# Sliding-window attention in steps of two query blocks, with the low key parts in the two row halves of TensorE

## The chip, the cores and the metric

The kernel runs on one core of one Trainium2 chip. The metric is the device time of one execution in microseconds (us), from its start to its end. The engines are named as in the profile: PE is TensorE (matrix products), PEld its loading of stationary operands ("weights"), DVE is VectorE, ACT is ScalarE, POOL is GpSimd, SP issues DMA transfers. PSUM is the memory that TensorE writes; it has eight banks of 512 float32 columns on 128 partitions. SBUF is the working memory that feeds the engines.

## The reference, cut to what matters

One transformer layer (D = 2048, 512 tokens): a root-mean-square norm, sliding-window attention with a gate, an output projection, then a second gated projection and a last norm. The change is inside the attention, which the reference computes per block of 128 queries against its own block of keys and the one before:

```python
q, k, v, gate = split(rmsnorm(x) @ w_in)     # 32 heads of q, 4 heads of k and v, 64 wide
scores = einsum('bnqhgd,bnjhd->bnhgqj', q, kb) * 64 ** -0.5 + bias
scores = where(mask, scores, min)            # 0 <= distance < 128
m = max(scores.max(-1), sink)
e = exp(scores - m)
probs = e / (e.sum(-1) + exp(sink - m))
out = einsum('bnhgqj,bnjhd->bnqhgd', probs, vb)
y = (out * silu(gate)) @ w_out
```

All of it is float32. The kernel gets close to that precision from products at the faster float32r rate by splitting each operand in a high part (rounded) and a low part (the rest), and adding the products high x high, low x high and high x low.

## The kernel before, in words

**Projections.** For each tile of 128 output columns, `mm3` (L113 to L115) runs three matmuls of 512 columns on each of 16 slices of D; three matmuls are one *projection slot*. `projections` (L592) is a generator that hands out one slot at a time: 30 tiles of q and of the gate, written to PSUM tag `p` (tiles qps and gps). The weights arrive by DMA in pieces of eight slices (wraw), ScalarE makes the high part whi (L99), VectorE the low part wlo (L100). When a tile of the gate is done, VectorE writes it to `gate` (L609); after four of them ScalarE applies silu (L404), which reloads its function table before and after.

**Attention in between.** Heads go in pairs (16 pairs c, of which four share a kv head), tokens in four blocks n. One step `i` is one pair and one block: 64 steps. The main loop (L631) runs `scores(i)`, then about seven projection slots, and `steps` (L621) puts `turn(i-1)` ahead of slot 4 and `weigh(i-2)` ahead of slot 6. The order on TensorE and of SP's transfers is the program's order; on the other engines a scheduler orders instructions by priority and data when the program is built, and each engine then runs its list in that order.

- `scores` (L304): for each head e of the pair, Q[c][e] holds that head's high part in one half of the 128 rows and its low part in the other half (even head: high in rows 0-63, odd head: high in rows 64-127). K holds the keys' high part in both halves, and the low part likewise. So one matmul of 128 rows against the high keys gives (high + low) q times high k. A second one against the low keys gives (high + low) q times low k. For block 0 there is one matmul of 256 columns per head (high and low side by side, L319), for blocks 1 to 3 two matmuls per head (L317). VectorE adds the bias (L326, sc), folds the two key blocks by a maximum (L332, t; exactly one of the two is unmasked at each position), takes the maximum over the row with the sink beside it (L337, sm); ScalarE takes the exponential with its sum (L340), VectorE divides (L341, L342). POOL writes the sink's column (L321).
- `turn` (L345): TensorE transposes t (L352, pt); ScalarE and VectorE split it in high and low (L354, L355: r); POOL cuts out the part that belongs to the query's own block (L360: own).
- `weigh` (L366): products with the values (L379); every second block ScalarE and VectorE combine the result to U (L385 to L388). POOL multiplies U into the gate later (L401, `gate_value`).

**Buffers.** PSUM has four tags p, s, t, o of two banks each. The scores use s, two buffers of one bank. In SBUF, t and sm have four buffers, r and own two.

**Weight sums.** `sum_weights` issues, a few in each step, copies (SP, L448) and adding copies (POOL queue, L450) that prepare sums of the later weights in DRAM.

**After the attention** the output projection begins (tiles o, banks s and p for the first product). Its weight pieces are split by ScalarE (L490, bhi) and VectorE (L491, blo), and VectorE combines quarters of `gate` (L572) for its operands.

Of the kernel before, what the change touches and what calls it, by code (L numbers as in the profile page):

```python
# [11 lines left out]
F32 = mybir.dt.float32  # L12
F32R = mybir.dt.float32r
# [36 lines left out]
def trunk_kernel(ctx: ExitStack, tc: tile.TileContext, a: dict):  # L50
    nc = tc.nc

    def pool(name, bufs=1, **kw):
        return ctx.enter_context(tc.tile_pool(name=name, bufs=bufs, **kw))
# [12 lines left out]
    acts = pool("acts", bufs=KC // 2)  # L67
    mid = ExitStack()
    more = mid.enter_context(tc.tile_pool(name="more", bufs=KC // 2))

    def quarter(name):
        return whole.tile([P, 4, S], F32, tag="quarter", name=name)

    def bank(name, tag):
        return psum.tile([P, 512], F32, tag=tag, name=name)


    WE = 1024
# [1 line left out]
    class Weights:  # L80
# [5 lines left out]
        def add(self, src):  # L86
            self.srcs.append(src)
# [204 lines left out]

    U, T, PT, O, gates, biases = {}, {}, {}, {}, {}, {}

    def load_bias(c):
# [3 lines left out]
        )  # L301
        nc.sync.dma_start(biases[c], src)

    def scores(i):  # L304


        c, n = divmod(i, NB)
        kv, nk = c // 4, 2 if n else 1
        if n == 0 and c + 1 < PAIRS:
            load_bias(c + 1)  # L310
        s_ps = bank(f"s{i}", "s").rearrange("p (u j) -> p u j", u=2)
        keys = slice(n + 1 - nk, n + 1)
        for e in range(2):
            st = Q[c][e][:, n * P : (n + 1) * P]
            if n:
                for low in range(2):
                    nc.tensor.matmul(s_ps[:, e, :], st, K[kv][:, keys, low], start=low == 0, stop=low == 1)  # L317
# [3 lines left out]
        nc.gpsimd.tensor_copy(t[:, :, 0], sinkb[:, 2 * c : 2 * c + 2])  # L321
        pr = t[:, :, 1:]
        sc = pr if n == 0 else apool.tile([P, 2, 2 * P], F32, tag="sc", name=f"sc{i}", bufs=1)

        def add(in0, in1):
            nc.vector.scalar_tensor_tensor(  # L326
                out=sc, in0=in0, scalar=sclq[:, n : n + 1], in1=in1, op0=ALU.mult, op1=ALU.add
            )

        if n:  # L330
            add(s_ps, biases[c][:, :, ::-1])
            nc.vector.tensor_max(pr, sc[:, :, :P], sc[:, :, P:])  # L332
        else:
            add(s_ps[:, :, :P], biases[c][:, :, :P][:, :, ::-1])
            add(s_ps[:, :, P:], sc)
        sm = apool.tile([P, 6], F32, tag="sm", name=f"sm{i}", bufs=4)
        nc.vector.tensor_reduce(sm[:, 0:2], t, axis=AX.X, op=ALU.max, negate=True)  # L337
        for e in range(2):
            te = t[:, e, :]
            nc.scalar.activation(te, te, AF.Exp, bias=sm[:, e : e + 1], accum_out=sm[:, 2 + e : 3 + e])  # L340
        nc.vector.reciprocal(sm[:, 4:6], sm[:, 2:4])  # L341
        nc.vector.tensor_mul(pr, pr, sm[:, 4:6].unsqueeze(2).to_broadcast([P, 2, P]))  # L342
        T[i] = t

    def turn(i):  # L345


        c, n = divmod(i, NB)
        t = T.pop(i)
        pt = bank(f"pt{i}", "t").rearrange("p (b u q) -> p b u q", b=2, u=2)[:, 0]  # L350
        for e in range(2):
            nc.tensor.transpose(pt[:, e, :], t[:, e, 1:], ident)  # L352
        r = apool.tile([P, 2, 2, P], F32R, tag="r", name=f"r{i}", bufs=2)
        nc.scalar.copy(r[:, 0], pt)  # L354
        nc.vector.tensor_sub(r[:, 1], pt, r[:, 0].bitcast(F32))  # L355
        own = None
        if n:
            own = apool.tile([P, 2, 2, P], F32R, tag="own", name=f"own{i}", bufs=2)
            flat = lambda v: v.rearrange("p l u q -> p (l u) q")
            nc.gpsimd.affine_select(  # L360
                out=flat(own), in_=flat(r).bitcast(F32), pattern=[[0, 4], [1, P]], compare_op=ALU.is_ge, fill=0.0,
                base=0, channel_multiplier=-1,
            )
        PT[i] = (r, own)

    def weigh(i):  # L366

        c, n = divmod(i, NB)
        kv = c // 4
        r, own = PT.pop(i)  # L370
        if n == 0:
            U[c] = apool.tile([P, S], F32, tag="u", name=f"u{c}", bufs=5)
        if n % 2 == 0:
            O[c] = bank(f"o{i}", "o").rearrange("p (b u q) -> p b u q", b=2, u=2)
        ops = O[c]
        parts = [(V[max(n - 1, 0)][:, kv], r)] + ([(DV[n][:, kv], own)] if n else [])
        for b, (st, pr) in enumerate(parts):
            for low in range(2):
                nc.tensor.matmul(  # L379
                    ops[:, n % 2], st, pr[:, low], start=b == low == 0, stop=low == 1 and b == len(parts) - 1  # L380
                )
        if n % 2 == 1:
            tmp = apool.tile([P, 2, P], F32, tag="tmp", name=f"tmp{i}", bufs=2)
            dst = U[c][:, (n - 1) * P : (n + 1) * P].rearrange("p (b q) -> p b q", b=2)
            nc.scalar.copy(tmp[0:64], ops[64:128, :, 0, :])  # L385
            nc.vector.tensor_add(dst[0:64], ops[0:64, :, 0, :], tmp[0:64])
            nc.scalar.copy(tmp[64:128], ops[0:64, :, 1, :])
            nc.vector.tensor_add(dst[64:128], ops[64:128, :, 1, :], tmp[64:128])  # L388
        if n == 3:
            weighed.add(c)  # L390
            if c in open_gates:
                due.append(c)
# [155 lines left out]
    class Forms:  # L548
# [6 lines left out]
        def steps(self, p):  # L555

            self.made[p] = []
            for h in range(2):
                a11, a21 = self.q[h][:, :, :256], self.q[h][:, :, 256:]
                a12, a22 = self.q[2 + h][:, :, :256], self.q[2 + h][:, :, 256:]  # L560
                if self.nm == "o":
                    src, sub = {
                        1: (a11, None), 7: (a11, (a21, a11)), 2: (a12, None), 6: (a11, (a22, a11)),
                        5: (a21, (a21, a22)), 3: (a12, (a12, a11)), 4: (a22, None),
                    }[p]
                else:
                    src, sub = {
                        2: (a12, None), 7: (a21, (a21, a11)), 1: (a11, None), 6: (a21, (a22, a21)),
                        5: (a11, (a11, a21)), 3: (a12, (a12, a21)), 4: (a22, None),
                    }[p]  # L570
                if sub:
                    nc.vector.tensor_sub(src, *sub)  # L572
# [42 lines left out]
    load_bias(0)  # L615
    for _ in range(KC):
        next(proj)
    blocks = PAIRS * NB
# [12 lines left out]
    for i in range(blocks):  # L631
        todo = left // (blocks - i)
        left -= todo
        scores(i)
        steps(i, todo)
        for n in range(i * SUM_STEPS // blocks, (i + 1) * SUM_STEPS // blocks):
# [327 lines left out]
```

## Time and profile before

| | |
|---|---|
| median of 3 runs | 835.68 us (832.84 to 836.26) |
| the profiled execution's own time | 835.59 us |
| its span, first to last instruction | 833.9 us |
| granted TensorE clock over the span | 0.990 |
| share of the span that PE, DVE, ACT, POOL are busy | 97%, 72%, 54%, 17% |
| attention stage | about 85 to 480 us |

How to read the rows. A *group* row gives line, engine, operation, the tile written and the tiles read, the shape and the count; then the busy time in us, the mean duration of one in ns, and the idle time of the engine just ahead of them with what ended it. A *timeline* row gives start and duration in us; "x2" merges two instructions, and the brackets hold the idle time before. A *wait* row reads "who <- for whom: us in total, times, longest". A row by *windows* gives for a stretch its length, then the busy time of PE, PEld, DVE, ACT and POOL with their counts, the granted clock, the share of DMA and GB/s. Matmuls are pipelined: one begins before the one ahead has ended, so the distance between two starts is what a matmul costs a busy TensorE.

### The profile page before, as it was taken

To read this page: it belongs to the slowest core of one execution; us is meant where nothing else is said; L and a number is where in the kernel's file an instruction comes from. 1 tells how busy PE (TensorE), PEld (TensorE's weight loads), DVE (VectorE), ACT (ScalarE), POOL (GpSimd) and SP (SyncE) were. 2 spreads that over 40 slices of the span, in tenths; PEclk is the share of its full clock that TensorE was granted. 3 is DMA by queue.
4 is the path that set the end of the run, shared out by engine and by line. 5 is a ranking of instruction groups with operands and counts; after the bars stand their busy time and mean duration, and the time that the engine had idled before them with its cause. 6 is when DMAs were issued, how large, how long until landed. Compare 5 with 4: busy or idle time off the path is not lost.

```text
span 833.9 us, 11252 instructions
## 1 busy us (share of the span) xinstructions
PE 811.3 (97%) x3972; PEld 679.1 (81%) x3972; DVE 599.4 (72%) x950; ACT 448.2 (54%) x860; POOL 145.5 (17%) x233
## 2 busy tenths in 40 slices
PE   8999999999999899999999988999999999999985
PEld 7888788888888788888888877888888888888874
DVE  3547877668787577768777877766656877769794
ACT  5734444644454554435644544554668856557664
POOL 1100211322222331212511130020000020202002
PEclk9999999999999999999999999999999999999998
DMA  8853767848577766776795277798521996875423
GB/s 292 305 190 111 192 190 234 215 151 219 146 216 233 215 196 195 214 166 174 205 277 164 76 274 280 261 301 220 194 84 51 371 203 208 184 212 185 151 87 116
DMA packets 45993, 165.98 MB, mean 199 GB/s; under 512 B 5440, under 2 KB 9696, under 8 KB 42096
## 3 DMA queue, kind: packets, MB, share of 16 engines
q1 hardware_dynamic: 38432, 129.52, 44.2%
q0 software_dynamic: 6928, 34.69, 21.9%
q10 hardware_dynamic: 576, 1.05, 0.4%
q8 instruction: 31, 0.51, 0.2%
q14 instruction: 26, 0.21, 0.1%
HBM read 160.99 MB, written 46.19 MB: 248 GB/s over the span
## 4 chain that ended last, share of the span: by engine, by line
PE 87%; DVE 5%; ACT 3%; DMA 2%; issue 1%; POOL 1%; SPq 0%; ACTq 0%; DVEq 0%
PE qps L114 7%; PE qps L113 7%; PE qps L115 7%; PE gps L113 6%; PE gps L115 6%; PE gps L114 6%; PE o L114 6%; PE o L115 6%; PE g L113 5%; PE o L113 5%; PE g L114 5%; PE g L115 5%; PE o L379 3%; PE s L317 2%; PE pt L352 2%
## 5 line engine op out<-in xcount | busy, mean ns | idle before, releaser
L491 DVE TENSOR_TENSOR blo<-braw,bhi 128x1024 fp32r<-128x1024 f32 x80 | 99.2, 1241 | 40.6 <-ACT bhi L490 40.4
L490 ACT CAST bhi<-braw 128x1024 fp32r<-128x1024 f32 x80 | 84.0, 1050 | 57.7 <-PE o L115 27.0
L340 ACT ACTIVATE t<-t,sm 128x129 f32<-128x129 f32 x128 | 50.6, 397 | 105.5 <-DVE sm L337 105.3
L113 PE MATMUL gps<-xh,whi 128*128 128x512 f32 x256 | 103.1, 403 | 0.0
L115 PE MATMUL gps<-xh,wlo 128*128 128x512 f32 x256 | 100.4, 392 | 0.0
L114 PE MATMUL gps<-xl,whi 128*128 128x512 f32 x256 | 100.4, 392 | 0.0
L100 DVE TENSOR_TENSOR wlo<-wraw,whi 128x1024 fp32r<-128x1024 f32 x60 | 75.1, 1251 | 29.3 <-ACT whi L99 28.3
L113 PE MATMUL qps<-xh,whi 128*128 128x512 f32 x224 | 91.1, 407 | 0.0
L114 PE MATMUL o<-blo,fho 128*128 128x512 f32 x224 | 88.0, 393 | 2.8 <-DVE blo L491 2.8
L113 PE MATMUL o<-bhi,fho 128*128 128x512 f32 x224 | 88.4, 395 | 1.5 <-ACT bhi L490 1.5
L115 PE MATMUL qps<-xh,wlo 128*128 128x512 f32 x224 | 88.3, 394 | 0.0
L114 PE MATMUL qps<-xl,whi 128*128 128x512 f32 x224 | 88.3, 394 | 0.0
L115 PE MATMUL o<-bhi,flo 128*128 128x512 f32 x224 | 88.0, 393 | 0.0
L99 ACT CAST whi<-wraw 128x1024 fp32r<-128x1024 f32 x60 | 62.7, 1045 | 36.6 <-DMA wraw<-in_w_gate_in 17.2
L113 PE MATMUL g<-bhi,fhg 128*128 128x512 f32 x208 | 81.3, 391 | 0.0
L115 PE MATMUL g<-bhi,flg 128*128 128x512 f32 x208 | 81.0, 389 | 0.0
L114 PE MATMUL g<-blo,fhg 128*128 128x512 f32 x208 | 80.9, 389 | 0.0
L491 DVE TENSOR_TENSOR blo<-grown,bhi 128x1024 fp32r<-128x1024 f32 x38 | 46.5, 1223 | 21.7 <-ACT bhi L490 21.2
L115 PEld LDWEIGHTS gps<-xh,wlo 128*128 128x128 f32 x256 | 48.1, 188 | 10.7
L114 PEld LDWEIGHTS gps<-xl,whi 128*128 128x128 f32 x256 | 48.3, 189 | 7.0
L490 ACT CAST bhi<-grown 128x1024 fp32r<-128x1024 f32 x38 | 39.9, 1050 | 26.0 <-PE o L115 11.0
L113 PEld LDWEIGHTS gps<-xh,whi 128*128 128x128 f32 x256 | 48.2, 188 | 6.9
(189 smaller groups left out, 1722.6 us busy)
## 6 DMA issues: line engine op xcount, KB each, us to landing
wraw<-in_w_gate_in SPq DMA_DIRECT2D x32, 512.0 KB, 6.1
wraw<-in_w_q SPq DMA_DIRECT2D x28, 512.0 KB, 7.1
w_out<-in_w_out POOLq DMA_DIRECT2D x24, 512.0 KB, 6.8
braw<-in_w_out SPq DMA_DIRECT2D x24, 512.0 KB, 3.2
braw<-in_ple_gate SPq DMA_DIRECT2D x24, 512.0 KB, 4.3
w_out<-in_w_out SPq DMA_DIRECT2D x16, 512.0 KB, 7.3
ple_gate<-in_ple_gate SPq DMA_DIRECT2D x16, 512.0 KB, 7.7
ple_gate<-in_ple_gate POOLq DMA_DIRECT2D x16, 512.0 KB, 7.7
```

Of the source, the lines that this page charges most:

```text
L99: nc.scalar.copy(hi, raw)
L100: nc.vector.tensor_sub(lo, raw, hi.bitcast(F32))
L113: nc.tensor.matmul(ps, sh, mh, start=first, stop=False, skip_group_check=more)
L114: nc.tensor.matmul(ps, sh, ml, start=False, stop=False, skip_group_check=more)
L115: nc.tensor.matmul(ps, sl, mh, start=False, stop=last, skip_group_check=more)
L317: nc.tensor.matmul(s_ps[:, e, :], st, K[kv][:, keys, low], start=low == 0, stop=low == 1)
L340: nc.scalar.activation(te, te, AF.Exp, bias=sm[:, e : e + 1], accum_out=sm[:, 2 + e : 3 + e])
L352: nc.tensor.transpose(pt[:, e, :], t[:, e, 1:], ident)
L379: nc.tensor.matmul(ops[:, n % 2], st, pr[:, low], start=b == low == 0, stop=low == 1 and b == len(parts) - 1)
L490: nc.scalar.copy(hi, raw)
L491: nc.vector.tensor_sub(lo, raw, hi.bitcast(F32))
```

## The change

The attention goes in 32 steps ("windows" w) of one pair and two blocks of queries (h = 0: blocks 0 and 1, h = 1: blocks 2 and 3). About 14 projection slots lie between two calls of `scores`; `turn(w-1)` stays ahead of slot 4, `weigh(w-2)` moves to slot 1, and in the last step back to slot 6. The products with the low parts of the keys use only the high part of q: 64 of the 128 rows, the even head in rows 0-63 and the odd head in rows 64-127. The product low q times low k is thereby left out. The two heads of a pair write to two different banks, so a window's scores take two banks as one buffer (`two_banks`), half a bank for each head and block. The exponentials stay one for each head and block; the maximum, the reciprocal, the division, the transposes' reading and the cut for the own block are one instruction for two blocks. t and sm have two buffers of twice the size or more, r and own one of twice the size. PSUM's pool ends with the attention, and a second one (`psum_late`) serves what follows; in it banks go to tags in the order of first use, and a tile waits for the earlier users of its bank.

```diff
-    psum = pool("psum", bufs=2, space=PSUM)
+    psum = [mid.enter_context(tc.tile_pool(name="psum", bufs=2, space=PSUM))]
...
+    def two_banks(name):
+        return psum[-1].tile([P, 2, 512], F32, tag="s", name=name, bufs=1)
...
-    kt_ps = [bank(f"ktps{t}", "s") for t in range(2)]
+    kt_both = two_banks("ktps")
+    kt_ps = [kt_both[:, t] for t in range(2)]
...
-        s_ps = bank(f"s{i}", "s").rearrange("p (u j) -> p u j", u=2)
-        keys = slice(n + 1 - nk, n + 1)
-        for e in range(2):
-            st = Q[c][e][:, n * P : (n + 1) * P]
+        s_ps = two_banks(f"s{w}").rearrange("p u (b j) -> p u b j", b=2)
+        for b in range(2):
+            n = 2 * h + b
+            cols = slice(n * P, (n + 1) * P)
+            if n == 0:
+                for e in range(2):
+                    nc.tensor.matmul(s_ps[:, e, b, :], Q[c][e][:, cols], K[kv][:, 0], start=True, stop=True)
+                continue
+            keys = slice(n - 1, n + 1)
+            for e in range(2):
+                nc.tensor.matmul(s_ps[:, e, b, :], Q[c][e][:, cols], K[kv][:, keys, 0], start=True, stop=False)
+            for e in range(2):
+                half = slice(64 * e, 64 * e + 64)
+                nc.tensor.matmul(
+                    s_ps[:, e, b, :], Q[c][e][half, cols], K[kv][half, keys, 1], start=False, stop=True
+                )
...
-            if n:
-                for low in range(2):
-                    nc.tensor.matmul(s_ps[:, e, :], st, K[kv][:, keys, low], start=low == 0, stop=low == 1)
-            else:
-                nc.tensor.matmul(s_ps[:, e, :], st, K[kv][:, 0], start=True, stop=True)
-        t = apool.tile([P, 2, 1 + P], F32, tag="t", name=f"t{i}", bufs=4)
+        t = apool.tile([P, 2, 2, 1 + P], F32, tag="t", name=f"t{w}", bufs=2)
...
-        sm = apool.tile([P, 6], F32, tag="sm", name=f"sm{i}", bufs=4)
-        nc.vector.tensor_reduce(sm[:, 0:2], t, axis=AX.X, op=ALU.max, negate=True)
-        for e in range(2):
+        sm = apool.tile([P, 24], F32, tag="sm", name=f"sm{w}", bufs=2)
+        flat = t.rearrange("p b u j -> p (b u) j")
+        nc.vector.tensor_reduce(sm[:, 0:4], flat, axis=AX.X, op=ALU.max, negate=True)
+        for e in range(4):
...
-        r = apool.tile([P, 2, 2, P], F32R, tag="r", name=f"r{i}", bufs=2)
+        r = apool.tile([P, 2, 2, 2, P], F32R, tag="r", name=f"r{w}")
...
-            own = apool.tile([P, 2, 2, P], F32R, tag="own", name=f"own{i}", bufs=2)
+        own = apool.tile([P, 2, 2, 2, P], F32R, tag="own", name=f"own{w}")
...
-    def steps(i, todo):
+    def steps(w, todo, at):
         for n in range(todo):
-            if n == 6 and 2 <= i < blocks + 2:
-                weigh(i - 2)
-            if n == 4 and 1 <= i < blocks + 1:
-                turn(i - 1)
-            if n == 5 and due:
+            if n == at and 2 <= w < windows + 2:
+                weigh(w - 2)
+            if n == 4 and 1 <= w < windows + 1:
+                turn(w - 1)
+            if n in (6, 10) and due:
                 gate_value()
...
+        steps(w, todo, 1)
+        for n in range(w * SUM_STEPS // windows, (w + 1) * SUM_STEPS // windows):
             sum_weights(n)
-    steps(blocks, 7)
-    steps(blocks + 1, 7)
+    steps(windows, 7, 1)
+    steps(windows + 1, 7, 6)
...
     late = pool("late", reuse_waits="tile")
+    psum.append(pool("psum_late", bufs=2, space=PSUM, reuse_waits="tile"))
```

More of the change, by code (lines that the diff above doesn't have):

```diff
@@ L74, in bank @@
     def bank(name, tag):
-        return psum.tile([P, 512], F32, tag=tag, name=name)
+        return psum[-1].tile([P, 512], F32, tag=tag, name=name)
+    def two_banks(name):
+        return psum[-1].tile([P, 2, 512], F32, tag="s", name=name, bufs=1)
     WE = 1024
@@ L302, in load_bias, with scores, add @@
         nc.sync.dma_start(biases[c], src)
[L304 to L309, printed above, removed]
+    def scores(w):
+        c, h = divmod(w, 2)
+        kv = c // 4
+        if h == 0 and c + 1 < PAIRS:
             load_bias(c + 1)
-        s_ps = bank(f"s{i}", "s").rearrange("p (u j) -> p u j", u=2)
-        keys = slice(n + 1 - nk, n + 1)
-        for e in range(2):
-            st = Q[c][e][:, n * P : (n + 1) * P]
+        s_ps = two_banks(f"s{w}").rearrange("p u (b j) -> p u b j", b=2)
[15 more added lines that the diff above has]
+        t = apool.tile([P, 2, 2, 1 + P], F32, tag="t", name=f"t{w}", bufs=2)
+        nc.gpsimd.tensor_copy(t[:, :, :, 0], sinkb[:, 2 * c : 2 * c + 2].unsqueeze(1).to_broadcast([P, 2, 2]))
+        for b in range(2):
+            n = 2 * h + b
+            pr = t[:, b, :, 1:]
+            sc = pr if n == 0 else apool.tile([P, 2, 2 * P], F32, tag="sc", name=f"sc{w}_{b}", bufs=1)
+            def add(in0, in1):
+                nc.vector.scalar_tensor_tensor(
+                    out=sc, in0=in0, scalar=sclq[:, n : n + 1], in1=in1, op0=ALU.mult, op1=ALU.add
+                )
@@ L337, in scores @@
-        nc.vector.tensor_reduce(sm[:, 0:2], t, axis=AX.X, op=ALU.max, negate=True)
-        for e in range(2):
[L339 to L352, printed above, removed]
-        r = apool.tile([P, 2, 2, P], F32R, tag="r", name=f"r{i}", bufs=2)
+                add(s_ps[:, :, b, :], biases[c][:, :, ::-1])
@@ new lines, in scores @@
+                nc.vector.tensor_max(pr, sc[:, :, :P], sc[:, :, P:])
+            else:
+                add(s_ps[:, :, b, :P], biases[c][:, :, :P][:, :, ::-1])
+                add(s_ps[:, :, b, P:], sc)
+        sm = apool.tile([P, 24], F32, tag="sm", name=f"sm{w}", bufs=2)
+        flat = t.rearrange("p b u j -> p (b u) j")
+        nc.vector.tensor_reduce(sm[:, 0:4], flat, axis=AX.X, op=ALU.max, negate=True)
+        for e in range(4):
+            te = flat[:, e, :]
+            nc.scalar.activation(te, te, AF.Exp, bias=sm[:, e : e + 1], accum_out=sm[:, 4 + e : 5 + e])
@@ new lines, in scores, with turn @@
+        nc.vector.reciprocal(sm[:, 8:12], sm[:, 4:8])
+        nc.vector.tensor_mul(flat[:, :, 1:], flat[:, :, 1:], sm[:, 8:12].unsqueeze(2).to_broadcast([P, 4, P]))
+        T[w] = t
+    def turn(w):
+        t = T.pop(w)
+        pt = bank(f"pt{w}", "t").rearrange("p (b u q) -> p b u q", b=2, u=2)
+        for b in range(2):
+            for e in range(2):
+                nc.tensor.transpose(pt[:, b, e, :], t[:, b, e, 1:], ident)
+        r = apool.tile([P, 2, 2, 2, P], F32R, tag="r", name=f"r{w}")
@@ L364, in turn, with weigh @@
-        PT[i] = (r, own)
-    def weigh(i):
-        c, n = divmod(i, NB)
+        own = apool.tile([P, 2, 2, 2, P], F32R, tag="own", name=f"own{w}")
+        flat = lambda v: v.rearrange("p l b u q -> p (l b u) q")
+        nc.gpsimd.affine_select(
+            out=flat(own), in_=flat(r).bitcast(F32), pattern=[[0, 8], [1, P]], compare_op=ALU.is_ge, fill=0.0,
+            base=0, channel_multiplier=-1,
+        )
+        PT[w] = (r, own)
+    def weigh(w):
+        c, h = divmod(w, 2)
         kv = c // 4
-        r, own = PT.pop(i)
-        if n == 0:
+        r, own = PT.pop(w)
+        if h == 0:
@@ L372, in weigh @@
             U[c] = apool.tile([P, S], F32, tag="u", name=f"u{c}", bufs=5)
[L373 to L389, printed above, removed]
+        ops = bank(f"o{w}", "o").rearrange("p (b u q) -> p b u q", b=2, u=2)
@@ new lines, in weigh @@
+        for b in range(2):
+            n = 2 * h + b
+            parts = [(V[max(n - 1, 0)][:, kv], r)] + ([(DV[n][:, kv], own)] if n else [])
+            for i, (st, pr) in enumerate(parts):
+                for low in range(2):
+                    nc.tensor.matmul(
+                        ops[:, b], st, pr[:, low, b], start=i == low == 0, stop=low == 1 and i == len(parts) - 1
+                    )
+        tmp = apool.tile([P, 2, P], F32, tag="tmp", name=f"tmp{w}", bufs=2)
+        dst = U[c][:, 2 * h * P : (2 * h + 2) * P].rearrange("p (b q) -> p b q", b=2)
@@ L390, in weigh @@
+        nc.scalar.copy(tmp[0:64], ops[64:128, :, 0, :])
+        nc.vector.tensor_add(dst[0:64], ops[0:64, :, 0, :], tmp[0:64])
+        nc.scalar.copy(tmp[64:128], ops[0:64, :, 1, :])
+        nc.vector.tensor_add(dst[64:128], ops[64:128, :, 1, :], tmp[64:128])
+        if h == 1:
             weighed.add(c)
@@ L617, in trunk_kernel @@
         next(proj)
-    blocks = PAIRS * NB
+    windows = PAIRS * NB // 2
     left = KC * (len(kinds) - 1) - 14
-    def steps(i, todo):
+    def steps(w, todo, at):
         for n in range(todo):
-            if n == 6 and 2 <= i < blocks + 2:
-                weigh(i - 2)
-            if n == 4 and 1 <= i < blocks + 1:
-                turn(i - 1)
-            if n == 5 and due:
+            if n == at and 2 <= w < windows + 2:
[3 more added lines that the diff above has]
+            if n in (6, 10) and due:
                 gate_value()
             next(proj)
-    for i in range(blocks):
-        todo = left // (blocks - i)
+    for w in range(windows):
+        todo = left // (windows - w)
         left -= todo
-        scores(i)
-        steps(i, todo)
-        for n in range(i * SUM_STEPS // blocks, (i + 1) * SUM_STEPS // blocks):
+        scores(w)
+        steps(w, todo, 1)
+        for n in range(w * SUM_STEPS // windows, (w + 1) * SUM_STEPS // windows):
             sum_weights(n)
-    steps(blocks, 7)
-    steps(blocks + 1, 7)
+    steps(windows, 7, 1)
+    steps(windows + 1, 7, 6)
     for _ in proj:
```

18 lines of the change are left out of this document (removed).

## The prediction

> **What bounds the kernel now.** I read the page's busy times first, then TensorE's waits, then its timeline inside one step of the attention, then the timelines around the two places where it stops.
>
> ```profile
> PE 811.3 (97%) x3972; PEld 679.1 (81%) x3972; DVE 599.4 (72%) x950; ACT 448.2 (54%) x860; POOL 145.5 (17%) x233
> ...
> PEclk9999999999999999999999999999999999999998
> ...
> PE pt L352 <- DVE t L342: 3.9, 2, 2.9
> PE o L114 <- DVE blo L491: 2.8, 2, 2.1
> ...
> 90.00:281.00 191.00, 190.03 (x968) 159.46 (x967) 143.06 (x276) 90.88 (x236) 44.37 (x80) 1.00 0.73 205
> 281.00:290.00 9.00, 6.10 (x24) 4.80 (x23) 4.85 (x11) 5.09 (x14) 5.72 (x6) 0.81 0.79 186
> 290.00:478.00 188.00, 188.00 (x957) 158.02 (x956) 143.84 (x272) 91.76 (x235) 45.19 (x73) 1.00 0.66 185
> ```
>
> TensorE is busy 97% of the span at an almost full clock. In the attention stage (90 to 478 us) its row is filled (190.03 of 191.00, 188.00 of 188.00), while VectorE (143.06 of 191.00) and ScalarE have room. So in this stage a matmul slot removed is time saved, and work on the other engines costs nothing until TensorE waits for it. It stopped there only for the transposes (L352), twice.
>
> **The slots.** Busy times of matmuls overlap, so I price by distances between starts.
>
> ```profile
> 208.53 0.39 PE L115 MATMUL gps<-xh,wlo 128*128 128x512 f32 x1
> 208.75 0.40 PE L317 MATMUL s<-K,qe 128*128 128x256 f32 x2
> 208.99 0.40 PE L317 MATMUL s<-K,qo 128*128 128x256 f32 x2
> 209.23 0.39 PE L113 MATMUL gps<-xh,whi 128*128 128x512 f32 x1
> 209.46 0.39 PE L114 MATMUL gps<-xl,whi 128*128 128x512 f32 x1
> ...
> L317 PEld LDWEIGHTS s<-K,qe x96: 187/188/188, 90.2 to 461.3; 128*128 128x128 f32 x96
> L317 PE MATMUL s<-K,qe x96: 277/280/283, 90.4 to 461.4; 128*128 128x256 f32 x96
> ```
>
> Four score matmuls of one block take 209.23 - 208.75 = 0.48 us, that is 0.12 us each, and a 512-column matmul 0.23 us. The two qe matmuls (keys high, keys low) are the x2 in one row.
>
> **The change, part by part.**
>
> *Low parts in row halves.* Before, blocks 1 to 3 of each of the 16 pairs (48 blocks) run four full matmuls. After, two full ones and two that use 64 rows each, head 0 in rows 0-63 and head 1 in rows 64-127, into different banks. The instructions are as many; if the two halves run at the same time, one slot in four goes: 48 x 0.12 = 5.8 us less. Block 0 has no low matmul and stays. No row of the trace shows a matmul on half the rows. Its gain is bounded by 5.8 us (full overlap) and 0 (no overlap); I take full overlap, since the operands lie in disjoint rows and the outputs in different banks. The full-to-half change of the array, 48 times in and 48 times out, is not in the trace either. The nearest rows are the transposes, another mode of the array, between full matmuls:
>
> ```profile
> 200.01 0.39 PE L115 MATMUL qps<-xh,wlo 128*128 128x512 f32 x1
> 200.24 0.38 PE L352 MATMUL pt<-ident,t 128*128 128x128 f32 x2
> 200.38 0.48 PE L113 MATMUL qps<-xh,whi 128*128 128x512 f32 x1
> 200.69 0.39 PE L114 MATMUL qps<-xl,whi 128*128 128x512 f32 x1
> ```
>
> The first transpose starts 0.23 us after the matmul ahead of it, the usual slot, so going over costs nothing. From 200.24 to 200.69 pass 0.45 us, of which the L113 matmul has 0.23: two transposes cost 0.22 us, 0.11 each, and coming back shows no extra. I take 0 for a switch. The upper end comes from the rows of one matmul: it lasts 0.28 us but gives up its slot after 0.12, so a full emptying of the array costs 0.16 us; if the next weights can only load after that (load at 208.53, matmul at 208.75, less what its slot hides: 0.12), 0.28 us. Over 96 switches that is 15.4 to 26.9 us, kept for a rival.
>
> *Two blocks a step.* Four transposes stand together instead of two and two; at 0.11 each that is equal. Weighing (L379) keeps its matmuls. So TensorE has no other term but its stops.
>
> ```profile
> 282.37 0.39 PE L115 MATMUL qps<-xh,wlo 128*128 128x512 f32 x1
> 285.66 0.66 PE L352 MATMUL pt<-ident,t 128*128 128x128 f32 x2 [2.90 <-DVE t L342]
> 285.97 0.78 PE L113 MATMUL qps<-xh,whi 128*128 128x512 f32 x1
> ...
> 288.25 0.63 PE L115 MATMUL qps<-xh,wlo 128*128 128x512 f32 x1
> 288.68 0.50 PE L379 MATMUL o<-r,V 128*128 128x256 f32 x2
> ...
> 93.41 0.39 PE L115 MATMUL gps<-xh,wlo 128*128 128x512 f32 x1
> 94.77 0.41 PE L352 MATMUL pt<-ident,t 128*128 128x128 f32 x2 [0.97 <-DVE t L342]
> ```
>
> At 282 us the transposes wait 3.29 - 0.23 = 3.1 us for t, and the next six matmuls run at the slow clock (granted 0.81 in that stretch): 285.97 to 288.68 is 2.71 us against 6 x 0.23, 1.3 us more. At 93 us 1.1 us goes. Together 5.5 us. Before, t has 7 + 4 = 11 projection slots (three matmuls, 0.69 us each) from its scores to its transposes, 7.6 us; after, 14 + 4 = 18, 12.4 us, plus the matmuls between. The work is this:
>
> ```profile
> L326 DVE SCALAR_TENSOR_TENSOR sc<-s,sclq,bias 128x512 f32<-128x512 f32 x48 | 35.8, 746 | 11.7 <-PE s L317 11.2
> L332 DVE TENSOR_TENSOR t<-sc 128x256 f32<-128x256 f32 x48 | 24.5, 510 | 1.6
> L337 DVE TENSOR_REDUCE sm<-t 128x2 f32<-128x258 f32 x64 | 27.0, 422 | 3.3 <-DVE t L326 0.5
> L342 DVE TENSOR_TENSOR t<-t,sm 128x256 f32<-128x256 f32 x64 | 28.7, 449 | 1.7
> L340 ACT ACTIVATE t<-t,sm 128x129 f32<-128x129 f32 x128 | 50.6, 397 | 105.5 <-DVE sm L337 105.3
> L340 ACT ACTIVATION_READ_ACCUMULATOR t<-t,sm 128x1 f32 x128 | 23.9, 187 | 0.0
> L360 POOL TENSOR_SCALAR_AFFINE_SELECT own<-r 128x512 fp32r<-128x512 f32 x48 | 33.6, 699 | 70.8 <-DVE r L355 70.8
> ...
> 278.00 1.28 ACT L404 ACT_TABLE_LOAD   x1
> 279.30 1.92 ACT L404 ACTIVATE gate<-gate 128x2048 f32<-128x2048 f32 x1
> 281.24 1.28 ACT L340 ACT_TABLE_LOAD   x1
> ```
>
> For two blocks at most 2 x (0.75 + 0.51 + 0.42 + 0.45) = 4.3 us of VectorE and four exponentials of 0.4 us (with their accumulator reads some 2.3 us), 6.6 us in line; the silu that held ScalarE for 4.5 us at 278 makes it 11.1, still under 12.4. I count both stops as gone: -5.5 us, with 0 as the other end, since weights that land late could hold ScalarE too. The scores' two banks are now one buffer: the next scores come 14 slots (9.7 us) later, the adds that free them take 2 x 0.75 us, so no wait. r and own are single: weighing a step stands at slot 1, the transposes that lead to the next r at slot 4 of the same step, 3 x 0.69 = 2.1 us later. Own doubles to some 1.4 us on POOL and has 11 slots, 7.6 us, from the transposes; what hides it is that POOL mostly waits for r (70.8 us idle in its row). If that cover goes, the weighing waits and everything on TensorE behind it. On SP and POOL the copies and adds of the weights are as many, issued after every 14 slots instead of every 7; they come in pairs more often, and only a late raw load would show it: 0 taken.
>
> *PSUM in two pools.* In the changed program the first output tile lies in the bank of the last gate projection, not in the scores' bank, so its first matmul waits for VectorE to read that projection. On VectorE the order also turns: the subtraction that waits for POOL (L572 on gate) stands ahead of the split of the fourth weight piece, no longer of the fifth.
>
> ```profile
> 483.55 6.03 POOL L401 TENSOR_TENSOR gate<-gate,u 128x512 f32<-128x512 f32 x4 [8.67 <-ACT gate L404]
> ...
> 489.62 1.23 DVE L572 TENSOR_TENSOR gate<-gate,gate 128x1024 f32<-128x1024 f32 x1 [3.69 <-POOL gate L401]
> 490.76 1.22 DVE L491 TENSOR_TENSOR blo<-braw,bhi 128x1024 fp32r<-128x1024 f32 x1
> ...
> 489.58 0.39 PE L113 MATMUL o<-bhi,fho 128*128 128x512 f32 x1
> 492.04 0.50 PE L114 MATMUL o<-blo,fho 128*128 128x512 f32 x1 [2.06 <-DVE blo L491]
> ```
>
> TensorE now stops at 489.58 for the fifth piece and goes on at 492.04. After, it stops one piece earlier, 12 matmuls or 2.7 us of work, and goes on at the same 492.04, because that moment is POOL's; the wait for the first bank is swallowed by it. So up to 2.7 us more, and a later stop for weights can return some: +2.0 taken, ends +0.3 and +4.0 (with a slow clock as at 282).
>
> **Sum.** Against the profiled execution's own 835.59 us (span 833.9; the median of the three runs shown, 835.68, is the same within 0.1): -5.8 - 5.5 + 2.0 = -9.3, so 826.3 us.
>
> **Rivals.** *Each switch empties the array* (the other side). For it: a matmul outlives its slot by 0.16 us. Against it: the transposes, which go over and back free. At 0.16 to 0.28 us a switch: 826.3 + 15.4 = 841.7 to 853.2 us. It decides from 9.3 / 96 = 0.097 us a switch on, and makes the kernel slower by over 0.5% from 0.14 us on. The Trainium skill, "TensorEngine Tiling (Array Packing)", Key Properties, says that changing the tiling mode, not just the tile, drains TensorE; by that rule this rival holds, and no run here shows it yet.
>
> *The halves don't overlap*, because each still loads 128 columns of weights: the load lasts 0.188 us, and transposes of 128 columns still take 0.11 us a slot as if a load set it. Then 832.1 us, within 0.5% (some 4.2 us, about what a measurement of this kernel can tell from no change). The Trainium skill's "TensorE: Matmul & The Clock Gate", section LDWEIGHTS, says that a load's time goes by columns, not rows, which speaks for this one.
>
> *A new wait in each step*: own or r late for the weighing. 0.3 us in each of 32 steps gives 826.3 + 9.6 = 835.9. Against it: the 7.6 us of lead.
>
> **How the numbers follow.** Forecast 0.40; switches empty the array 0.38; no overlap 0.15; new waits 0.07. I predict 826.3. Faster by over 0.5% (under 831.5): nearly all of the first and a little of the third, 0.42. Within: most of the third, the edges of the others, 0.17. Slower (over 839.9): the second and some of the last, 0.41. Range 823 to 850: down to a better end than the sum by 3 us, up to 0.25 us a switch. The forecast's own range is 823 to 831.
>
> **What would show it.** Right: row-half matmuls starting within some 0.02 us of each other, the slot after them 0.12 us later, no stop at the third silu, a stop of some 3 us at the fourth weight piece near 478 us. Wrong: gaps of 0.16 us or more ahead of the first half and of the next full matmul, 96 times; halves 0.12 us apart; TensorE waiting for own or r.

## The result, and the profile after

The changed kernel takes 843.9 us (median of 4 runs, 842.26 to 845.7); the kernel before, beside it, 834.68 us. The ratio is 1.0112, with an interval of 1.008 to 1.0143: 1.1% slower, where 826.3 us, faster than before, was predicted. The profiled execution took 843.93 us, with a span of 842.2 us.

The busy times on the page of the changed kernel, then two rows of TensorE's waits, the only two that lie in the attention or at its end, then its windows (length of the stretch, then busy time and count of PE, PEld, DVE, ACT and POOL, granted clock, share of DMA, GB/s):

```profile
PE 822.1 (98%) x3972; PEld 681.4 (81%) x3972; DVE 581.7 (69%) x822; ACT 443.3 (53%) x828; POOL 147.7 (18%) x185
```

```profile
PE o L392 <- POOL own L373: 2.1, 1, 2.1
...
PE o L116 <- DVE gate L621: 1.9, 1, 1.9
```

```profile
90.00:281.00 191.00, 191.00 (x948) 157.02 (x946) 133.35 (x209) 88.35 (x219) 45.66 (x56) 1.00 0.74 204
281.00:290.00 9.00, 9.00 (x43) 7.20 (x42) 4.45 (x8) 4.94 (x12) 5.30 (x6) 1.00 0.74 197
```

Up to 290 us TensorE waits less than before (191.00 of 191.00 and 9.00 of 9.00 busy, where 190.03 and 6.10 stood), and the waits for t are gone from the list; the two waits above come later. Yet from 90 to 281 us it gets through 948 matmuls where 968 stood, at a full clock. So in this stretch the time went into matmuls, not into waits. The timeline of TensorE in one step of two blocks, blocks 2 and 3, shows which:

```profile
215.34 0.28 PE L326 MATMUL s<-K,qe 128*128 128x256 f32 x1
215.45 0.28 PE L326 MATMUL s<-K,qo 128*128 128x256 f32 x1
215.66 0.38 PE L329 MATMUL s<-K,qe 64*128 64x256 f32 x1
215.67 0.38 PE L329 MATMUL s<-K,qo 64*128 64x256 f32 x1
215.98 0.38 PE L326 MATMUL s<-K,qe 128*128 128x256 f32 x1
216.20 0.28 PE L326 MATMUL s<-K,qo 128*128 128x256 f32 x1
216.41 0.38 PE L329 MATMUL s<-K,qe 64*128 64x256 f32 x1
216.41 0.38 PE L329 MATMUL s<-K,qo 64*128 64x256 f32 x1
216.72 0.50 PE L116 MATMUL gps<-xh,whi 128*128 128x512 f32 x1
217.06 0.39 PE L117 MATMUL gps<-xl,whi 128*128 128x512 f32 x1
```

The two halves start within 0.01 us of each other, so they do overlap. But from the last full product to the halves pass 0.21 us instead of 0.12, from the halves to the next full product 0.31 instead of 0.12, and that full product gives up its slot only after 0.22 (216.20 - 215.98) or, with 512 columns, 0.34 (217.06 - 216.72) instead of 0.12 and 0.23. The second block takes 216.72 - 215.98 = 0.74 us for three slots, where four slots took 0.48. Three slots are 0.36 us, so two switches cost 0.38 us, 0.19 each. The loads of weights (PEld) of the same stretch show a part of the reason:

```profile
215.34 0.19 PEld L326 LDWEIGHTS s<-K,qo 128*128 128x128 f32 x1
215.66 0.18 PEld L329 LDWEIGHTS s<-K,qe 64*128 64x128 f32 x1
215.67 0.18 PEld L329 LDWEIGHTS s<-K,qo 64*128 64x128 f32 x1
215.98 0.19 PEld L326 LDWEIGHTS s<-K,qe 128*128 128x128 f32 x1
216.09 0.19 PEld L326 LDWEIGHTS s<-K,qo 128*128 128x128 f32 x1
```

Inside one tiling a load runs one matmul ahead: that of qo at 215.34 is for the matmul at 215.45. The loads behind a switch stand at the start of their own matmul (215.66, 215.98), and the one after them comes 0.11 us later. No load is fetched across the switch.

The balance of the attention stage, from its first score matmul to the first output matmul; the first two rows are of the kernel before, the others of the changed one:

```profile
85.40 0.28 PE L319 MATMUL s<-K,qe 128*128 128x256 f32 x1
...
478.69 0.40 PE L113 MATMUL o<-bhi,fho 128*128 128x512 f32 x1
```

```profile
84.88 0.28 PE L322 MATMUL s<-K,qe 128*128 128x256 f32 x1
...
487.14 0.50 PE L116 MATMUL o<-bhi,fho 128*128 128x512 f32 x1 [1.93 <-DVE gate L621]
...
497.68 0.50 PE L117 MATMUL o<-blo,fho 128*128 128x512 f32 x1 [0.27 <-DVE blo L503]
```

393.3 us became 402.3; ahead of the stage 0.5 us less, and behind its end as much as before (833.9 - 478.69 = 355.2, 842.2 - 487.14 = 355.1). Summed over all distances between starts in the stage, the scores with the first matmul behind them cost 13.0 us more. If 48 slots (5.8 us) are saved, as the four pairs below bear out, the 96 switches cost 18.8 us (0.196 us each). The stops at 93 and 282 us are gone (-5.5). A new stop for own adds 2.3 to the distances, the wait for the first output bank 2.1, and the projections run 2.3 us faster (last section). That makes 9.6 of 9.0 us; the transposes and the weighing cost the other 0.6 less.

The new stop, first on TensorE, then on GpSimd:

```profile
413.48 0.50 PE L392 MATMUL o<-own,DV 128*128 128x256 f32 x2 [2.13 <-POOL own L373]
```

```profile
407.45 4.74 POOL L413 TENSOR_TENSOR gate<-gate,u 128x512 f32<-128x512 f32 x3 [1.41 <-ACT gate L416]
412.15 1.27 POOL L373 TENSOR_SCALAR_AFFINE_SELECT own<-r 128x1024 fp32r<-128x1024 f32 x1
```

Three products of the gate, released together by the third silu, stand ahead of the cut for the own block on GpSimd; VectorE had written r at 408.56 us, and the cut began at 412.15.

### The profile page after: what moved, and what is told of

It reads as the page before. It is cut to its first block, busy times and chain, and to the rows that moved or that the text cites. A ratio compares the mean times of both kernels' runs of the same rounds, so it can differ in the third digit from the quotient of the medians.

```text
span 842.2 us, 10996 instructions
## 1 busy us (share of the span) xinstructions
PE 822.1 (98%) x3972; PEld 681.4 (81%) x3972; DVE 581.7 (69%) x822; ACT 443.3 (53%) x828; POOL 147.7 (18%) x185
## 4 chain that ended last, share of the span: by engine, by line
PE 91%; DVE 3%; DMA 2%; ACT 2%; POOL 1%; issue 1%; SPq 0%; DVEq 0%; ACTq 0%
PE gps L116 7%; PE qps L116 7%; PE gps L117 7%; PE gps L118 7%; PE qps L117 7%; PE qps L118 7%; PE o L117 5%; PE o L116 5%; PE o L118 5%; PE g L117 5%; PE g L118 5%; PE g L116 5%; PE o L392 3%; PE s L329 2%; PE s L326 2%; PE pt L367 2%
## 5 line engine op out<-in xcount | busy, mean ns | idle before, releaser
L116 PE MATMUL gps<-xh,whi 128*128 128x512 f32 x256 | 103.1, 403 | 0.0
L116 PE MATMUL o<-bhi,fho 128*128 128x512 f32 x224 | 88.9, 397 | 3.5 <-DVE gate L621 1.9
L116 PE MATMUL qps<-xh,whi 128*128 128x512 f32 x224 | 90.8, 405 | 0.0
L116 PE MATMUL g<-bhi,fhg 128*128 128x512 f32 x208 | 81.3, 391 | 0.0
L397 ACT COPY tmp<-o 64x256 f32<-64x256 f32 x32 | 11.9, 370 | 99.9 <-PE o L392 99.8
L116 PEld LDWEIGHTS gps<-xh,whi 128*128 128x128 f32 x256 | 48.1, 188 | 10.3
```

The lines of the kernel that those rows point to most:

```text
L116: nc.tensor.matmul(ps, sh, mh, start=first, stop=False, skip_group_check=more)
```

## The experiments

The theory: a change between whole array and row halves costs about 0.196 us, whatever runs beside it. The rivals: the two-block steps, the seam or two halves running together make the kernel slow. "The changed kernel" is the one of the diff above. The kernel before took 833.22 us (median) beside the kernels on full rows, with the halves alone, regrouped and with the banks of before; 833.14 beside the lone half, the four pairs and the shared gates; 835.04 beside the last.

**Low products on full rows.** The low products use all rows again, which undoes the switches and puts low q times low k back in; all else stays.

```diff
-                half = slice(64 * e, 64 * e + 64)
                 nc.tensor.matmul(
-                    s_ps[:, e, b, :], Q[c][e][half, cols], K[kv][half, keys, 1], start=False, stop=True
+                    s_ps[:, e, b, :], Q[c][e][:, cols], K[kv][:, keys, 1], start=False, stop=True
                 )
```

> The changed kernel with the low key products on all 128 rows again (low q times low k is back in); the two-block steps, the buffers and the two PSUM pools stay. If the price lies in the 96 switches between whole array and row halves (each about 0.2 us by the distances in the changed kernel's timeline, less the 5.8 us that the overlap gives), 13 us go: about 831 us, faster than before by 0.4 to 0.5%. If the two-block steps with their single buffers are what costs, it stays at 843 to 844.

Measured: 832.21 us, ratio 0.9986 (0.9968 to 1.0005). The stage takes 391.5 us, its score slots are 0.12 us again (eight in 212.87 - 211.92 = 0.95 us), and the distances between score starts sum to 26.6 us as before the change (26.5; the changed kernel 36.1):

```profile
211.92 0.28 PE L326 MATMUL s<-K,qe 128*128 128x256 f32 x1
...
212.87 0.40 PE L116 MATMUL gps<-xh,whi 128*128 128x512 f32 x1
```

So the loss lies in the halves; the two-block steps, the single buffers and the seam together leave the kernel where it was or slightly faster. That is 1.2 us more than the 831 us expected; in this kernel TensorE's stop for own is 2.7 us.

**Halves alone.** The kernel before, in steps of one block, with only the halves, the two banks that they need, and the second PSUM pool with its banks given out as before.

```diff
...
+                nc.tensor.matmul(s_ps[:, e, :], Q[c][e][:, cols], K[kv][:, keys, 0], start=True, stop=False)
...
+        if n:
+            for e in range(2):
+                half = slice(64 * e, 64 * e + 64)
+                nc.tensor.matmul(
+                    s_ps[:, e, :], Q[c][e][half, cols], K[kv][half, keys, 1], start=False, stop=True
+                )
...
```

> The kernel before, one block a step, with the row halves alone; the scores take two banks as one buffer, and PSUM gets its second pool with the banks given out in the old order. If the switches cost: 13 us over before, about 848 us. If the two-block steps cost: at most before, or 829 us with the overlap's 5.8 us gained.

Measured: 849.22 us, ratio 1.0197 (1.0164 to 1.023). In its timeline full product to halves takes 0.21 us, halves to the next full one 0.31, as in the changed kernel, so the price does not come from the two-block step. It loses 16.0 us, more than the changed kernel: its scores' tile has one buffer and steps half as long, and a wait of 1.8 us for it (s behind VectorE's reading, once, at 92 us) is new. The rest of the difference is not assigned.

**A lone half.** Head 1's low product on full rows, head 0's alone in a row half: the same 96 switches, no overlap, no slot saved.

```diff
-            for e in range(2):
-                half = slice(64 * e, 64 * e + 64)
+            for e in (1, 0):
+                half = slice(0, P) if e else slice(0, 64)
```

> From the changed kernel: the low product of head 1 runs on all 128 rows again, and that of head 0 alone stays in rows 0 to 63, so a block of scores has the sequence full, full, full, one half. There are still two changes between whole array and row half in each of the 48 blocks, but no two halves run beside each other and no slot is saved. If a change of the row tiling is what costs (my theory, 0.196 us each from the changed kernel's trace), this costs 96 x 0.196 = 18.8 us more than the kernel with all products on full rows (832.2 us): about 851 us, slower than the changed kernel, with the start of the half some 0.21 us behind the full product ahead of it and the next full one some 0.3 us behind the half. If the cost comes from two halves being in the array together (the rival: the two weight loads or the two results get in each other's way), a lone half costs a slot of 0.11 to 0.12 us like any other, and the time is about 832 us.

Measured: 848.57 us (one run). Its TensorE timeline:

```profile
218.35 0.38 PE L326 MATMUL s<-K,qe 128*128 128x256 f32 x1
...
218.90 0.38 PE L329 MATMUL s<-K,qe 64*128 64x256 f32 x1
219.21 0.50 PE L116 MATMUL gps<-xh,whi 128*128 128x512 f32 x1
```

The block takes 219.21 - 218.35 = 0.86 us, four slots of 0.12 and the same 0.38 for two switches. Two halves in each other's way are excluded: one half alone costs the same. In this trace the scores with the first matmul behind them take 18.2 us more than in that of the kernel on full rows (52.3 against 34.1), 0.19 for each of 96 switches. The whole run lost only 16.4 us instead of 18.8; its stop for own is 0.8 us shorter, and the rest is not assigned.

**Halves regrouped.** In the second block of a step the halves go first, so the halves of blocks 2 and 3 stand together: 64 switches instead of 96, the same products.

```diff
+            for half_rows in ((False, True) if b == 0 else (True, False)):
+                for e in range(2):
+                    rows = slice(64 * e, 64 * e + 64) if half_rows else slice(0, P)
+                    first = half_rows == (b == 1)
+                    nc.tensor.matmul(
+                        s_ps[:, e, b, :], Q[c][e][rows, cols], K[kv][rows, keys, int(half_rows)], start=first, stop=not first
+                    )
```

> The changed kernel with the order turned in the second block of a step (low halves first, then the high products), so that the halves of both blocks stand together: 64 switches instead of 96, the same products. If a switch costs about 0.2 us: 32 x 0.196 = 6.3 us less, about 837.6 us. If the switches are free and something else costs: 843 to 844 us.

Measured: 838.8 us, ratio 1.0063 (1.0035 to 1.009). Against the changed kernel's ratio that is 0.5%, some 4 us, for 32 switches fewer, against 6.3 us by 0.196 each. The distance to the kernel on full rows, 6.6 us, is what 64 switches (12.5) less 48 slots (5.8) make, 6.7. The traces say it more sharply than the times: the scores with the first matmul behind them take 40.7 us instead of the changed kernel's 47.0, that is 6.3 us for 32 switches. The price follows the number of switches.

**Four pairs of halves.** What does a pair cost inside an array that is already split?

```diff
-            for e in range(2):
+            for again in range(4):
+                for e in range(2):
...
-                    s_ps[:, e, b, :], Q[c][e][half, cols], K[kv][half, keys, 1], start=False, stop=True
+                        s_ps[:, e, b, :], Q[c][e][half, cols], K[kv][half, keys, 1], start=False, stop=again == 3
```

> From the changed kernel: each pair of halves is issued four times in a row instead of once, so the low products are added three times too often and the scores are not the reference's; only the time of the added pairs counts. Nothing is switched between the four pairs, so the three added ones give the price of a pair inside an already split array. If the halves overlap fully, with their loads ahead as on the whole array, a pair takes a slot of 0.118 us: 3 x 48 x 0.118 = 17 us, about 861 us. If two halves go one after the other even so, each pair takes two slots, 0.22 us: 32 us, about 876 us. If each pair waits for its own loads (0.18 us for the 128 columns) before it can start, 0.29 to 0.31 us a pair: 42 to 45 us, about 887 us. The regrouped kernel's second pair stood 0.22 us behind its first, but that one still followed a switch; the third and fourth pairs here do not.

Measured: 856.25 us (one run), 12.3 more than the changed kernel's profiled execution. Its TensorE timeline, of each pair the row of qe:

```profile
221.49 0.28 PE L326 MATMUL s<-K,qo 128*128 128x256 f32 x1
221.70 0.38 PE L330 MATMUL s<-K,qe 64*128 64x256 f32 x1
...
221.93 0.28 PE L330 MATMUL s<-K,qe 64*128 64x256 f32 x1
...
222.04 0.28 PE L330 MATMUL s<-K,qe 64*128 64x256 f32 x1
...
222.16 0.28 PE L330 MATMUL s<-K,qe 64*128 64x256 f32 x1
...
222.37 0.39 PE L326 MATMUL s<-K,qe 128*128 128x256 f32 x1
222.59 0.28 PE L326 MATMUL s<-K,qo 128*128 128x256 f32 x1
```

The third and fourth pair follow after 0.11 to 0.12 us: two halves cost one slot, full overlap. Each switch is seen in its two parts. The first matmul of the new tiling starts 0.21 us behind the last of the old one (221.49 to 221.70, 222.16 to 222.37), 0.09 too late; and it holds its own slot 0.22 us (221.70 to 221.93, 222.37 to 222.59), 0.10 too long. Its loads show the second part:

```profile
221.70 0.18 PEld L330 LDWEIGHTS s<-K,qe 64*128 64x128 f32 x1
...
221.81 0.19 PEld L330 LDWEIGHTS s<-K,qe 64*128 64x128 f32 x1
...
221.93 0.18 PEld L330 LDWEIGHTS s<-K,qe 64*128 64x128 f32 x1
```

The second pair's load comes only at 221.81, 0.11 us behind the first, and its matmul 0.12 us later; the third pair's load, at 221.93, is again a matmul ahead (222.04). A single pair between two switches shows 0.21 and 0.31: the long slot and the late start fall together. The three added pairs cost 17.0 us in the scores' distances (36.1 to 53.1), as full overlap had it. The whole is only 12.3: 4.4 us come back behind the attention, where TensorE ran at a better clock, and the stop for own is 0.7 us shorter. The windows that begin at the first output matmul, of the changed kernel and of this one (the clock stands third from the end):

```profile
487.10:520.00 32.90, 30.25 (x116) 23.94 (x117) 22.30 (x24) 14.64 (x15) 5.56 (x5) 0.90 0.68 260
```

```profile
503.80:537.00 33.20, 29.99 (x128) 23.98 (x129) 23.22 (x25) 15.77 (x16) 5.57 (x5) 1.00 0.70 269
```

At a clock of 0.90 instead of 1.00 the changed kernel gets through 12 matmuls fewer in nearly the same time, by estimate some 2.5 us of the 4.4.

**Banks as before.** On full rows; the second PSUM pool gives its banks to the tags in the order of before, so that the first output tile does not wait for the last gate projection.

```diff
     psum.append(pool("psum_late", bufs=2, space=PSUM, reuse_waits="tile"))
+    for tag in "ps":
+        for n in range(2):
+            bank(f"first_{tag}{n}", tag)
```

> As e1 with the second PSUM pool's banks given out in the old order, so that the first output product finds its banks free. If that first wait (1.9 us) is a cost of its own: 829 us. If it only takes the place of a stop at the fourth weight piece, whose split stands behind the wait for POOL on VectorE: a stop of 2 to 3 us appears there and the time is that of e1, 831 us.

Measured: 830.7 us, ratio 0.9972 (0.9952 to 0.9992). TensorE's timeline around the fourth weight piece:

```profile
482.61 0.39 PE L116 MATMUL o<-bhi,fho 128*128 128x512 f32 x1
487.05 0.79 PE L117 MATMUL o<-blo,fho 128*128 128x512 f32 x1 [4.05 <-DVE blo L502]
```

VectorE's, in the same stretch:

```profile
484.63 1.22 DVE L583 TENSOR_TENSOR gate<-gate,gate 128x1024 f32<-128x1024 f32 x1 [5.32 <-POOL gate L412]
```

The wait of 1.9 us for the bank is gone, and a stop of 4.05 us at the fourth piece stands in its place; the time differs from that of the kernel on full rows (832.21 us) by no more than the intervals allow. So I read the two as one loss in two places, of which the earlier, where it is, takes time from the later. VectorE waits there 5.32 us for GpSimd's products of the gate.

**Gate products shared.** The kernel of the run above (full rows, banks as before), with two of the last four products on VectorE.

```diff
-        nc.gpsimd.tensor_mul(src, src, U[c])
+        engine = nc.vector if c in (13, 15) else nc.gpsimd
+        engine.tensor_mul(src, src, U[c])
```

> From the kernel with the low products on full rows and the banks of before: in the last group of gates, two of the four products gate times u (pieces 13 and 15) are taken by VectorE instead of GpSimd, nothing else. If the stop of TensorE at the fourth piece of weights of the third stage (4.0 us in that kernel) is the queue of GpSimd's products of 1.2 to 1.6 us each, which VectorE's sum of the gate waits for, two of them less end it about 3 us sooner: 827.5 to 828 us, ratio to before about 0.992 to 0.993, and the stop at that piece falls to about 1 us. If VectorE itself, with its own work of that stretch, is what is late, the two added products of some 0.6 us each leave the time at 830.7 or up to 1 us above.

Measured: 829.7 us, ratio 0.9951 (0.9934 to 0.9969). The stop falls from 4.05 to 2.53 us, and the slow clock behind it goes (granted clock 0.50 from 487 to 490 us there, 1.00 from 474 to 500 us here). That it got shorter shows GpSimd's queue in it; less than the 3 us expected, since GpSimd's two products took 1.75 us each. And a stop for a later piece is new (2.3 us behind ScalarE's bhi), so most is given back. The difference to the run above, 0.2%, is not resolved.

**Own freed.** Also the products of pairs 10 and 11 on VectorE, so that two instead of three stand ahead of own.

```diff
-        engine = nc.vector if c in (13, 15) else nc.gpsimd
+        engine = nc.vector if c in (10, 11, 13, 15) else nc.gpsimd
```

> From the kernel before this one: of the third group of gates, VectorE also takes the products of pairs 10 and 11, so that GpSimd has two products ahead of the cut for the own block instead of three, and none is added ahead of it. If the stop of TensorE at 400 us in front of the weighing (2.7 us for own, and 1.3 to 1.6 us of slow clock behind it) is GpSimd's queue, it falls to under 1.5 us or goes, and the attention ends some 2 to 4 us sooner. If that time is kept, 826 to 827.5 us; if the stage behind the attention gives it back, since its weights and its splits are no earlier (as most of the gain at the fourth piece was given back by a stop of 2.3 us at the start of a later piece), 829 to 830 us with longer stops for blo or bhi there. If own is late for another reason, the stop stays at 2.7 us.

Measured: 829.55 us, ratio 0.9949 (0.9931 to 0.9967): no gain. The timeline of all engines around TensorE's stop in this kernel, and (second fence) the cut for the own block in the kernel of the run above:

```profile
398.20 3.50 POOL L413 TENSOR_TENSOR gate<-gate,u 128x512 f32<-128x512 f32 x2 [1.91 <-ACT gate L416]
...
400.48 2.30 DVE L103 TENSOR_TENSOR wlo<-wraw,whi 128x1024 fp32r<-128x1024 f32 x1
...
401.65 2.08 POOL L372 TENSOR_SCALAR_AFFINE_SELECT own<-r 128x1024 fp32r<-128x1024 f32 x1
...
403.79 0.50 PE L391 MATMUL o<-own,DV 128*128 128x256 f32 x2 [2.21 <-POOL own L372]
```

```profile
401.39 1.27 POOL L372 TENSOR_SCALAR_AFFINE_SELECT own<-r 128x1024 fp32r<-128x1024 f32 x1
```

One product less stood ahead, but the cut itself took 2.08 us instead of 1.27, beside VectorE's split of weights, which took 2.30. The stop only went from 2.7 to 2.2 us. So the queue is part of it; that the slowing of two engines beside each other is the rest is read from the rows, not tested by itself. This kernel and the two before it are all faster than the kernel before the change, by 0.3 to 0.5%; between the last two there is no difference.

## Why the prediction was wrong

*"I take 0 for a switch"* is the step that failed. A switch costs 0.19 to 0.20 us, 18.8 us in all; with it the prediction's own sum is 845.1, against 843.9 measured. That the two are so near is partly luck: the stop for own (+2.3) and the faster projections (-2.3) stood in no sum and cancel. The first rival had the switch, at 0.16 to 0.28 us and a chance of 0.38 against the forecast's 0.40. The nearest row that was chosen, the transposes, is no such change: a transposing matmul of 128x128 fills all rows, and its load runs ahead like any other (in the trace of the kernel before, the load at 200.01 us, the matmul at 200.24). The rows that bore on it were the rival's: a matmul lasts 0.16 us beyond its slot, and a load that may not run ahead adds to it. By these rows the load adds 0.22 - 0.12 = 0.10 us, so the rival's upper end should have been 0.26, not 0.28. The 0.10 came out as the slot held too long; the late start is 0.09, less than the 0.16.

The Trainium skill, "TensorEngine Tiling (Array Packing)", Key Properties, says that changing the tiling mode drains TensorE. The trace agrees in that every switch costs time, 0.19 us, with a lone half as well. It does not show the emptying itself: the first half starts 0.21 us behind a matmul whose row lasts 0.28.

*48 x 0.12 for the saved slots* was right: the halves start together, and a pair in a split array costs 0.11 to 0.12 us.

*The halves don't overlap* fell with it. The Trainium skill, "TensorE: Matmul & The Clock Gate", section LDWEIGHTS, says that a load's time goes by columns; the rows agree (0.18 us on 64 rows, 0.19 on 128). What does not follow is that two halves take turns: their loads start at 215.66 and 215.67 and run beside each other.

*The stops for t, -5.5,* were right in place and size: both are gone, and the stretch of the third silu, 281 to 290 us, is filled (9.00 of 9.00).

*Four transposes at 0.11* was right:

```profile
220.54 0.60 PE L367 MATMUL pt<-ident,t 128*128 128x128 f32 x4
220.89 0.47 PE L116 MATMUL gps<-xh,whi 128*128 128x512 f32 x1
221.21 0.39 PE L117 MATMUL gps<-xl,whi 128*128 128x512 f32 x1
```

From 220.54 to 221.21 pass 0.67 us, less 0.23 for L116: 0.44 for four.

*What hides own is that POOL mostly waits for r* held 31 times and failed once. The row with 70.8 us of idle time is a sum over the stage; at 411 us the products released by the silu stood ahead, 4.74 us, and TensorE lost 2.3. The third rival was right in kind, in one step instead of 32.

*The seam, +2.0,* was right in size (1.9 us of waiting ahead of the first output matmul, and behind it the same time as before within 0.1) and wrong in form: a wait for the bank ahead of the first matmul and 0.27 us at the fourth piece, not some 3 us there. The prediction had the later stop swallow the earlier wait; the earlier took the later's time. The banks of before brought the predicted stop back, at 4.05 us.

## What to carry to other kernels

A change of the row tiling costs two parts that a busy TensorE does not show otherwise, a late start (0.09 us) and a first slot held too long, because the next load did not run ahead (0.10 us): here 0.19 us, more than a slot of 0.12 us. By these numbers, for matmuls of 256 columns, splitting the array pays only where more than three pairs of halves (3 x 0.12 us against 2 x 0.19) follow each other between two full products; no run here shows such a gain. So group them first and count the switches, not the slots. For the price of an operation that no trace shows, a row that looks alike (the transposes) must share the property that is priced, here the rows of the array that are in use.

## What was not expected

- No load of weights runs ahead across a switch (the rows at 215.66 and 215.98 above), though inside either tiling, whole or split, it does (216.09 in the changed kernel, 221.93 in the four pairs). What holds it back is not shown.
- Matmuls of 512 columns run slightly slower behind an interruption. In the changed kernel's timeline, five slots behind the weighing and five far from one:

```profile
218.47 0.39 PE L116 MATMUL gps<-xh,whi 128*128 128x512 f32 x1
...
219.63 0.39 PE L118 MATMUL gps<-xh,wlo 128*128 128x512 f32 x1
...
222.36 0.39 PE L116 MATMUL qps<-xh,whi 128*128 128x512 f32 x1
...
223.49 0.39 PE L118 MATMUL qps<-xh,wlo 128*128 128x512 f32 x1
```

  1.16 us against 1.13 for five. With three interruptions in each of 32 steps instead of 64, 96 fewer times 5 x 5 ns make by estimate some 2.4 us; 2.3 were found. The cause was not tried.
- GpSimd's cut for the own block took 1.27 us, or 2.08 us where VectorE split weights beside it (the two fences of the last run). The Trainium skill, "SBUF — State Buffer", section Who interferes with whom, says that a VectorE instruction with two SBUF inputs contends with a GpSimd instruction that reads SBUF; the split of weights is one with two inputs, so the rows agree. No run here separates it from other causes.
